# Hybrid diffusion backbone on one core: the output projection by Strassen's method, gating's normalisation on ScalarE, the second modulation in three parts

## The chip, the core and the metric

The kernel runs on one core of a Trainium2 chip. The core has a matmul engine (TensorE, PE in the profile; its weight loads are PEld), a vector engine (VectorE, DVE), a scalar engine (ScalarE, ACT), a general engine (GpSimd, POOL) and a queue that issues DMAs (SyncE, SP). They run side by side and wait for each other by semaphores. The metric is the device time of one execution in microseconds; it is given as a median over several runs.

## The reference

One layer of a token mixer with a convolutional channel mixer, over 512 latent tokens of width 1024 and 256 context tokens. Cut to what matters here:

```python
sh1x, sc1x, g1x, sh2x, sc2x, g2x = split(silu(c) @ w_ada + b_ada, 6)
z = h @ w_in;  u, vs, q, r, ga, gb, k, v, lr = split(z)
a = gelu(u) * (einsum('gpq,bnqgc->bnpgc', sgu_w, layer_norm(gelu(vs))) + sgu_b)   # spatial gating
ob = rms_norm(gated_linear_attention(q, k, v, lr)) * silu(r)
merged = sigmoid(ga) * (a @ w_br_a) + sigmoid(gb) * (ob @ w_br_b)
x = x + g1x * (merged @ w_o)                       # the output projection
hx2 = rms_norm(x) * norm2_g * (1 + sc2x) + sh2x    # second modulation
x = x + g2x * conv_ffn(hx2)                        # up, 3x3 convolution, gelu, down
return rms_norm(x) * final_norm_g
```

The six vectors of the modulation are 1024 long; the first two (sh1, sc1) are made at the start of the kernel, g1, sh2, sc2 and g2 later. `w_ada` is 1024 x 6144.

## The kernel before

All products are made with operands split into a high part (type fp32r) and a low part, and three matmuls for each product: high by high, high by low, low by high. A matmul has a 128 x 128 stationary block and up to 512 moving columns. The high part of a weight is made by ScalarE (L138, `A.copy`), the low part by VectorE (L139, a subtraction); `stream_load` and `stream_split` fetch and split weights some places ahead of their use, in the order of the list `specs`. A raw weight has 4 buffers, a split one 5 (`wh`, `wl`).

The program is written as one sequence. A scheduler of the language orders it for each engine when it is built, by the tiles that the instructions read and write and by the order in the text; an engine then runs its own instructions strictly in that order. Tiles come from pools: `heap` (44 of 2 KB a partition), `late` (27), and the eight PSUM banks as `mm` (4) and `gl` (4). A DMA on SP's queue that needs a tile which isn't free holds up all DMAs behind it.

The stages around the change, in the order in which they run:

- **vs and u.** `wide_tm` makes vs, its gelu is kept in eight `late` tiles `vraw`. After the mean and variance of all tokens are known, 32 operations of VectorE (L1104) write the normalised `vsn`, 128 x 128 each. Then for each of eight column blocks of u: 24 matmuls (`prod_cm`), gelu on ScalarE, and one block later `sgu_part`, the gating with `vsn`.
- **The second modulation** (`ada2`) is a generator that runs in the background: each `tick` takes it one step further. It makes eight accumulators of 512 columns in two parts of four (g1 and sh, then sc and g2). One step fetches a 128 x 512 piece of `w_ada` and adds it, scaled by c, to an accumulator (L1125, VectorE), 32 such steps a part; then each accumulator is split, summed over partitions by two matmuls (L1131, L1132) and copied to a broadcast tile (g1, g2) or turned into a column (sh, sc). Ticks are placed in u, in branch a, in branch b and in the output projection, 80 in all.
- **Branch a** (`wide_kk`, 192 matmuls). Beside it `hx_sums` makes the sums that Strassen's method needs of the input (L1205 to L1226).
- **ga, gb and r** are made by `strassen` on the transposed input: seven products of 24 matmuls in place of eight. The sums of the weights are made partly by DMAs that add into a tile (`add_rows`, POOL's queue), partly by VectorE (L211, L213). In `strassen` a result that takes part in several outputs is copied between banks by ScalarE and combined by VectorE (L453, L459).
- **Branch b** (`wide_tm`, 192 matmuls). Its output tile (t, hf), token tile t of four and column half hf, is multiplied by the gate and added to branch a (L1321, L1322), then put on a list `todo`; `turn` transposes it (four 128 x 128 transposes) and splits it into `mg`, which the output projection reads.
- **The output projection** (`wide_tm`, 192 matmuls). Each output (t, hf) is scaled by g1 and added to x (L1384, L1385), squared and summed on ScalarE (L1386). When both halves of a token tile are there, `norm2_tok` makes its root and scales it, and for each pair of token tiles `norm2_half` transposes (L1371), modulates on ScalarE (L1376) and splits on VectorE (L1379, L1380) into `h2`.
- **Up.** 44 products of 24 matmuls with `h2`. The first four are made on the token half 0 first, 256 columns wide, then on half 1; from block 2 on all 512 columns at once. Behind each pair of products VectorE makes the convolution: eight taps (L1430), then a product with the gelu (L1432). **Down** follows, by Strassen's method too.

Of the kernel before, what the change touches and what calls it, by code (L numbers as in the profile page):

```python
# [8 lines left out]
F32 = mybir.dt.float32  # L9
# [4 lines left out]
ALU = mybir.AluOpType  # L14
# [19 lines left out]
def backbone_kernel(  # L34
# [26 lines left out]
    def late(shape, dt=F32, s="l"):  # L61
        return lp.tile(shape, dt, tag="l", name=nm(s))
# [107 lines left out]

    def w_strassen(w, c0):

# [34 lines left out]
        def split_t2(j):  # L207
            def split():
                r11, r12 = raws["b11k", j], raws["b12", j]
                for kk in range(2):  # L210
                    V.tensor_tensor(tt[j][kk], tt[j][kk], r11[:, kk, :], op=ALU.add)  # L211
# [16 lines left out]
        for o, fs in ((0, [load_raw("b11", 0, 0, j) for j in js]), (2, [load_t(j) for j in js]),  # L228
                      (4, [load_raw("b12", 0, 1, j) for j in js]), (6, [load_raw("b21", 1, 0, j) for j in js]),
                      (10, [load_raw("b22", 1, 1, j) for j in js])):  # L230
            loads.extend((base + o + j, fs[j]) for j in js)
# [18 lines left out]
    w_wide(w_br_b[0], scaled=True)  # L250
    w_wide(w_o[0])
    for f in range(FT):
# [153 lines left out]

    def wide_tm(acts, done, step):
# [3 lines left out]
        for t in range(4):  # L411
            ps = (mm if t else gl)()
# [11 lines left out]
    def strassen(acts, done, step):  # L424

        def prod(ps, name, again):
            for j in range(2):
                wh, wl = weights(3, 6)
                for t in range(2):
                    for kk in range(2):  # L430
                        ah, al = (z[:, t * P:(t + 1) * P] for z in acts[name][2 * j + kk])
                        first = j == 0 and kk == 0 and not again
                        for i, (a, b) in enumerate(((ah, wh), (ah, wl), (al, wh))):
                            T.matmul(ps[t], a, b[:, kk, :], start=(first and i == 0),  # L434
                                     stop=(j == 1 and kk == 1 and i == 2), skip_group_check=again)
                step()
# [664 lines left out]
    vrs, ors = var[:, 0, :], var[:, 1:5, :]  # L1101
    for g in range(8):
        for t in range(4):
            V.tensor_scalar(vsn[g][:, t, :], vraw[g // 4][t][:, (g % 4) * P:(g % 4 + 1) * P], mv[:, t, 0:1],  # L1104
                            vrs[:, t:t + 1], op0=ALU.subtract, op1=ALU.mult)

# [3 lines left out]

    def ada2():
        for part in range(2):
            acc = []
            for j in range(4):
                a_ = late([P, 512], s="acc")
                G.memset(a_, 0.0)
                c0 = 2048 + part * 2048 + j * 512
                dma(a_[0:1, :], b_ada[0:1, c0:c0 + 512])
                acc.append(a_)
            for k in range(KT):  # L1120
                for j in range(4):
                    c0 = 2048 + part * 2048 + j * 512
                    w_ = late([P, 512], s="wa2")
                    dma(w_, w_ada[0, k * P:(k + 1) * P, c0:c0 + 512])
                    V.scalar_tensor_tensor(acc[j], w_, cs[:, k, 0:1], acc[j], op0=ALU.mult, op1=ALU.add)  # L1125
                    yield
            for j in range(4):
                ah, al = split_act(acc[j], s="acc")
                yield
                ps = gl()  # L1130
                T.matmul(ps, ones_r, ah, start=True, stop=False)  # L1131
                T.matmul(ps, ones_r, al, start=False, stop=True)  # L1132
                kind = ("g1", "sh", "sc", "g2")[part * 2 + j // 2]
                if kind in ("g1", "g2"):
                    t_ = late([P, 512], s=kind)
                    A.copy(t_, ps)
                    bc_g[kind, j % 2] = t_
                else:
                    t_ = heap([P, 4, P], s="dg")
                    V.tensor_tensor(t_, ps.rearrange("p (b r) -> p b r", b=4),  # L1140
                                    ident.unsqueeze(1).to_broadcast([P, 4, P]), op=ALU.mult)
                    if kind not in cols:
                        cols[kind] = const([P, 8], "col_" + kind)
                    V.reduce_sum(cols[kind][:, (j % 2) * 4:(j % 2) * 4 + 4], t_, axis=AX.X)
                yield

# [47 lines left out]
    def hx_sums():  # L1194
# [6 lines left out]
        for k in range(4):  # L1201
            u, v = heap([P, 512], s="hu"), heap([P, 512], s="hv")
            s1, q, s3, s4 = u[:, :256], u[:, 256:], v[:, :256], v[:, 256:]
            for d, (h, l), (h_, l_) in ((s1, a22[k], a21[k]), (s3, a11[k], a21[k])):
                V.tensor_tensor(d, f_(h), f_(h_), op=ALU.subtract)  # L1205
                V.tensor_tensor(s4, f_(l), f_(l_), op=ALU.subtract)
# [146 lines left out]

    xs_t = []

    am2 = const([P, 8], "am2")

    def norm2_cols():
        drain()
        V.tensor_scalar(am2, cols["sc"], 1.0, None, op0=ALU.add)  # L1360
        V.tensor_tensor(am2, am2, n2g, op=ALU.mult)
# [19 lines left out]

    def wo_done(hf, t, ps):
        tmp = late([P, 512], s="yt")
        V.tensor_tensor(tmp, ps, bc_g["g1", hf], op=ALU.mult)  # L1384
        V.tensor_tensor(x1[t][hf], x1[t][hf], tmp, op=ALU.add)  # L1385
        A.activation(tmp, x1[t][hf], AF.Square, accum_out=ss2[:, t, hf:hf + 1])  # L1386
        if hf == 1:
            xs_t.append(norm2_tok(t))
            if t >= 2:
                norm2_half(t - 2)  # L1390

    count[0] = 0

    def wo_step():
        count[0] += 1
        do()
        tick(2)
        if count[0] == KT:
            norm2_cols()

    wide_tm(of_blocks(mg), wo_done, wo_step)

# [324 lines left out]
```

## Time and profile before

| | us |
|---|---|
| median of 3 runs | 930.67 |
| runs | 930.3 to 932.23 |
| the profiled execution | 931.34 |
| its span, first to last instruction | 929.6 |

| stage | from, to (us of the span) |
|---|---|
| u, with gating | about 262 to 314 |
| branch a | 314 to 357.6 |
| ga, gb, r | 357.6 to 473.5 |
| branch b | 473.5 to 530 |
| output projection | 530 to 573 |
| up | 573 to 815 |
| down and the final norm | 815 to 929.6 |

The profile is of one execution. Its page gives busy time for each engine, the chain of work that ended last and the costliest groups of instructions by line. Other views of the same trace used below are the waits, the chain in order of time, the timeline of one engine, and windows (busy time of each engine in a stretch, with the clock granted to PE and the share of time that the DMA engines were busy). A row of instructions reads: start, time, engine, line, operation, output<-inputs, count, and in brackets the engine's idle time before it with what ended it.

### The profile page before, as it was taken

To read this page: it belongs to the slowest core of one execution; us is meant where nothing else is said; L and a number is where in the kernel's file an instruction comes from. 1 tells how busy PE (TensorE), PEld (TensorE's weight loads), DVE (VectorE), ACT (ScalarE), POOL (GpSimd) and SP (SyncE) were. 2 spreads that over 40 slices of the span, in tenths; PEclk is the share of its full clock that TensorE was granted. 3 is DMA by queue.
4 is the path that set the end of the run, shared out by engine and by line. 5 is a ranking of instruction groups with operands and counts; after the bars stand their busy time and mean duration, and the time that the engine had idled before them with its cause. 6 is when DMAs were issued, how large, how long until landed. Compare 5 with 4: busy or idle time off the path is not lost.

```text
span 929.6 us, 12825 instructions
## 1 busy us (share of the span) xinstructions
PE 907.7 (98%) x4695; PEld 761.1 (82%) x4695; DVE 755.2 (81%) x1349; ACT 447.8 (48%) x787; POOL 52.8 (6%) x80
## 2 busy tenths in 40 slices
PE   6999999999999999999999999999999999999996
PEld 5776898988878888888878888988888888878885
DVE  5567758689689978866789987798888888999797
ACT  5136546457443337755652334543333333366574
POOL 3000000000000011112100000000000000132000
PEclk9999999999999999999999999999999999999998
DMA  9940411132077384885649642333333333399432
GB/s 275 336 130 24 136 47 46 46 96 64 23 228 231 112 227 90 230 212 144 187 127 340 228 142 78 102 94 95 109 92 91 93 109 110 85 251 246 127 101 91
DMA packets 123547, 130.06 MB, mean 140 GB/s; under 512 B 6953, under 2 KB 84085, under 8 KB 123485
## 3 DMA queue, kind: packets, MB, share of 16 engines
q1 hardware_dynamic: 114781, 115.75, 40.2%
q0 software_dynamic: 6976, 12.28, 8.0%
q10 hardware_dynamic: 1728, 1.22, 0.4%
q8 instruction: 37, 0.61, 0.3%
q14 instruction: 25, 0.20, 0.1%
HBM read 127.13 MB, written 2.10 MB: 139 GB/s over the span
## 4 chain that ended last, share of the span: by engine, by line
PE 82%; DVE 10%; ACT 2%; DMA 2%; issue 2%; SPq 1%; ACTq 0%; DVEq 0%
PE mm L361 27%; PE mm L387 13%; PE gl L434 7%; PE gl L1532 6%; PE mm L434 5%; PE mm L1532 4%; PE gl L387 4%; PE gl L876 3%; PE mm L380 3%; DVE cacc L1430 2%; PE mm L372 1%; PE mm L666 1%; PE mm L980 1%; DVE bc L844 1%; DVE wl L139 1%
## 5 line engine op out<-in xcount | busy, mean ns | idle before, releaser
L138 ACT CAST wh<-raw 128x1024 fp32r<-128x1024 f32 x110 | 115.4, 1052 | 148.8 <-PE mm L361 99.8
L139 DVE TENSOR_TENSOR wl<-raw,wh 128x1024 fp32r<-128x1024 f32 x110 | 133.9, 1220 | 43.7 <-ACT wh L138 43.3
L361 PE MATMUL mm<-h2h,wh 128*128 128x512 f32 (+1 forms) x352 | 133.5, 379 | 0.0
L361 PE MATMUL mm<-h2l,wh 128*128 128x512 f32 (+1 forms) x352 | 133.5, 379 | 0.0
L361 PE MATMUL mm<-h2h,wl 128*128 128x512 f32 (+1 forms) x352 | 133.5, 379 | 0.0
L1430 DVE SCALAR_TENSOR_TENSOR cacc<-ca,ccol,cacc 128x441 f32<-128x441 f32 (+2 forms) x176 | 121.7, 695 | 4.1
L361 PEld LDWEIGHTS mm<-h2h,wh 128*128 128x128 f32 x352 | 66.2, 188 | 12.5
L361 PEld LDWEIGHTS mm<-h2l,wh 128*128 128x128 f32 x352 | 66.2, 188 | 12.4
L361 PEld LDWEIGHTS mm<-h2h,wl 128*128 128x128 f32 x352 | 66.2, 188 | 12.4
L1125 DVE SCALAR_TENSOR_TENSOR acc<-wa,cs,acc 128x512 f32<-128x512 f32 x64 | 45.1, 744 | 2.1 <-DMA wa<-in_w_ada_dram 2.1
L387 PE MATMUL mm<-wh,trh 128*128 128x512 f32 x112 | 44.4, 397 | 0.0
L387 PE MATMUL mm<-wh,trl 128*128 128x512 f32 x112 | 44.0, 392 | 0.0
L387 PE MATMUL mm<-wl,trh 128*128 128x512 f32 x112 | 43.7, 390 | 0.0
L1431 ACT ACTIVATE cacc<-cacc 128x512 f32<-128x512 f32 x22 | 13.9, 633 | 58.5 <-DVE cacc L1430 58.5
L361 PE MATMUL mm<-hxh,wh 128*128 128x512 f32 x104 | 41.7, 401 | 0.0
L361 PE MATMUL mm<-hxh,wl 128*128 128x512 f32 x104 | 41.0, 394 | 0.0
L361 PE MATMUL mm<-hxl,wh 128*128 128x512 f32 x104 | 40.7, 391 | 0.0
L1474 ACT CAST wh<-raw 128x1024 fp32r<-128x1024 f32 x22 | 23.0, 1052 | 20.5 <-PE mm L1532 6.1
L1454 POOL DMA_DIRECT2D b<-in_ffn_w_down_dram x11 | 9.4, 878 | 370.5 <-DMA b<-in_ffn_w_down_dram 356.8
L1475 DVE TENSOR_TENSOR wl<-raw,wh 128x1024 fp32r<-128x1024 f32 x22 | 26.8, 1219 | 4.4 <-ACT wh L1474 4.3
L186 POOL DMA_DIRECT2D tt<-in_w_in_dram x24 | 20.9, 1135 | 166.2 <-DVE hu L1207 77.5
L434 PE MATMUL mm<-wh,hxh 128*128 128x512 f32 x72 | 28.0, 389 | 0.0
(489 smaller groups left out, 2323.5 us busy)
## 6 DMA issues: line engine op xcount, KB each, us to landing
raw<-in_w_in_dram SPq DMA_DIRECT2D x54, 512.0 KB
wa<-in_w_ada_dram SPq DMA_DIRECT2D x96, 256.0 KB
raw<-in_ffn_w_up_dram SPq DMA_DIRECT2D x44, 512.0 KB
raw<-in_ffn_w_down_dram SPq DMA_DIRECT2D x22, 512.0 KB
tt<-in_w_in_dram POOLq DMA_DIRECT2D x24, 256.0 KB, 7.7
raw<-in_w_br_a_dram SPq DMA_DIRECT2D x8, 512.0 KB
raw<-in_w_br_b_dram SPq DMA_DIRECT2D x8, 512.0 KB
raw<-in_w_o_dram SPq DMA_DIRECT2D x8, 512.0 KB
```

What stands on the lines that cost most here:

```text
L138: A.copy(wh, raw)
L139: V.tensor_tensor(wl, raw, wh.bitcast(F32), op=ALU.subtract)
L361: T.matmul(ps, a[:, k, :], b[:, c0:c0 + n], start=(k == 0 and i == 0), stop=(k == KT - 1 and i == 2))
L380: T.matmul(ps, a[:, t * P:(t + 1) * P], b[:, k % 4, :], start=(k == 0 and i == 0), stop=(k == KT - 1 and i == 2))
L387: T.matmul(ps, a, b[:, k % 2, :], start=(k == 0 and i == 0), stop=(k == KT - 1 and i == 2))
L434: T.matmul(ps[t], a, b[:, kk, :], start=(first and i == 0), stop=(j == 1 and kk == 1 and i == 2), skip_group_check=again)
L876: T.matmul(ps, p_, q_, start=(start and z == 0), stop=(stop and z == 2))
L1125: V.scalar_tensor_tensor(acc[j], w_, cs[:, k, 0:1], acc[j], op0=ALU.mult, op1=ALU.add)
L1430: V.scalar_tensor_tensor(o, a_[:, r0 + dy:r1 + dy, c0 + dx:c1 + dx], wcol(tap), o, op0=ALU.mult, op1=ALU.add)
L1474: A.copy(wh, raw)
L1475: V.tensor_tensor(wl, raw, wh.bitcast(F32), op=ALU.subtract)
L1532: T.matmul(ps, a[:, t * P:(t + 1) * P], w[b][:, j, c0:c0 + n], start=(first and i == 0), stop=(last and i == 2), skip_group_check=again)
```

## The change

- The output projection is made by `strassen` in place of `wide_tm`. Its weights come from `w_strassen`, with a new option: b12 + b11 is made by a DMA that adds (`load_b12`), not by VectorE.
- The sums of the merged branches that it needs are made in `mg_turn` behind the same transposes as before, as the outputs of branch b come. For that the second half of branch b goes through the token tiles in the order 2, 0, 3, 1.
- The outputs of the projection now come in the order that `strassen` gives: (t 0, 1; hf 0), (2, 3; 1), (2, 3; 0), (0, 1; 1). The norm of tiles 2 and 3 is therefore made first, and up's first products are made on token half 1 first.
- `vsn` is written by ScalarE, four operations a block, one block ahead of its use, and no longer all at once by VectorE.
- `ada2` runs in three parts: g1 and sh, then sc, both with more ticks in u and branch a and finished before the projection (`drain`), and g2 with one tick a block in up. Its high parts are made by ScalarE.
- `hx_sums` joins high and low parts first (two additions of 512 columns) and then makes its sums, 6 operations a block in place of 10.

```diff
+        def load_b12(j):
+            def load():
+                load_raw("b12", 0, 1, j)()
+                if add_b12:
+                    G.dma_start(raws["b12", j], blk(0, 0, j).rearrange("(k p) c -> p k c", p=P), accum_op=ALU.add)
...
                 w = split_t(j)
-                V.tensor_tensor(r12, r12, raws.pop(("b11k", j)), op=ALU.add)
+                raws.pop(("b11k", j))
+                if not add_b12:
+                    V.tensor_tensor(r12, r12, r11, op=ALU.add)
                 add_rows(j, 1, 0)
...
-    w_wide(w_o[0])
+    w_strassen(w_o[0], 0, True)
...
     A.activation(var, var, AF.Sqrt, bias=eps_t, scale=1.0)
     V.reciprocal(var, var)
     vrs, ors = var[:, 0, :], var[:, 1:5, :]
-    for g in range(8):
+    vnb = const([P, 4], "vnb")
+    V.scalar_tensor_tensor(vnb, mv[:, :, 0], -1.0, vrs, op0=ALU.mult, op1=ALU.mult)
+
+    def vs_norm(g):
         for t in range(4):
-            V.tensor_scalar(vsn[g][:, t, :], vraw[g // 4][t][:, (g % 4) * P:(g % 4 + 1) * P], mv[:, t, 0:1],
-                            vrs[:, t:t + 1], op0=ALU.subtract, op1=ALU.mult)
+            A.activation(vsn[g][:, t, :], vraw[g // 4][t][:, (g % 4) * P:(g % 4 + 1) * P], AF.Identity,
+                         bias=vnb[:, t:t + 1], scale=vrs[:, t:t + 1])
 
 
...
+    def ada2(kinds):
+        cs0 = {"g1": 2048, "sh": 3072, "sc": 4096, "g2": 5120}
+        todo_ = [(kind, j, cs0[kind] + j * 512) for kind in kinds for j in range(2)]
...
+            for a_, (_, _, c0) in zip(acc, todo_):
+                w_ = late([P, 512], s="wa2")
+                dma(w_, w_ada[0, k * P:(k + 1) * P, c0:c0 + 512])
+                V.scalar_tensor_tensor(a_, w_, cs[:, k, 0:1], a_, op0=ALU.mult, op1=ALU.add)
                 yield
...
-    bg.append(ada2())
+    bg.extend([ada2(("g1", "sh")), ada2(("sc",))])
...
-        tick(2)
+        if j < KT - 1:
+            vs_norm(j + 1)
+        tick(2 + j % 2)
...
-            for d, (h, l), (h_, l_) in ((s1, a22[k], a21[k]), (s3, a11[k], a21[k])):
-                V.tensor_tensor(d, f_(h), f_(h_), op=ALU.subtract)
-                V.tensor_tensor(s4, f_(l), f_(l_), op=ALU.subtract)
-                V.tensor_tensor(d, d, s4, op=ALU.add)
-            V.tensor_tensor(q, s1, f_(a11[k][0]), op=ALU.add)
-            V.tensor_tensor(q, q, f_(a11[k][1]), op=ALU.add)
-            V.tensor_tensor(s4, q, f_(a12[k][0]), op=ALU.subtract)
-            V.tensor_tensor(s4, s4, f_(a12[k][1]), op=ALU.subtract)
+            f1, f2 = heap([P, 512], s="hf"), heap([P, 512], s="hf")
+            V.tensor_tensor(f1, f_(hx[k][0]), f_(hx[k][1]), op=ALU.add)
+            V.tensor_tensor(f2, f_(hx[4 + k][0]), f_(hx[4 + k][1]), op=ALU.add)
+            V.tensor_tensor(s1, f2[:, 256:], f1[:, 256:], op=ALU.subtract)
+            V.tensor_tensor(s3, f1[:, :256], f1[:, 256:], op=ALU.subtract)
+            V.tensor_tensor(q, s1, f1[:, :256], op=ALU.add)
+            V.tensor_tensor(s4, q, f2[:, :256], op=ALU.subtract)
...
-            tick(2)
+            tick(3 if count[0] <= KT else 4)
...
+    def mg_turn(t, hf):
+
+        s_, u, f_ = gb[t][hf], t % 2, lambda z: z.bitcast(F32)
+
+        def split(name, src, scale=1.0):
+            hi, lo = heap([P, 512], F32R, s="mh"), heap([P, 512], F32R, s="ml")
+            if scale == 1.0:
+                A.copy(hi, src)
+                V.tensor_tensor(lo, src, f_(hi), op=ALU.subtract)
+            else:
+                A.mul(hi, src, scale)
+                V.scalar_tensor_tensor(lo, src, scale, f_(hi), op0=ALU.mult, op1=ALU.subtract)
+            mg[name, u] = hi, lo
+
+        def go():
+            ps = gl()
+            for kk in range(4):
+                T.matmul(ps[:, kk * P:(kk + 1) * P], s_[:, kk * P:(kk + 1) * P], ident, is_transpose=True,
+                         start=kk == 0, stop=kk == 3, skip_group_check=True)
+            if t > 1 and hf == 0:
+                mf["a21", u] = heap([P, 512], s="mf")
+                A.copy(mf["a21", u], ps)
+            elif hf == 0:
+                mf["a11", u] = heap([P, 512], s="mf")
+                A.copy(mf["a11", u], ps)
+                split("a11", ps)
+                d = heap([P, 512], s="ms")
+                V.tensor_tensor(d, ps, mf["a21", u], op=ALU.subtract)
+                split("s3", d)
+            elif t > 1:
+                split("a22", ps)
+                d, q = mf.pop(("a21", u)), mf["a11", u]
+                V.tensor_tensor(d, ps, d, op=ALU.subtract)
+                V.tensor_tensor(q, q, d, op=ALU.add)
+                split("s2", q, -1.0)
+                split("s1", d)
+            else:
+                split("a12", ps)
+                q = mf.pop(("a11", u))
+                V.tensor_tensor(q, q, ps, op=ALU.subtract)
+                split("s4", q)
+        return go
...
-        todo.append(turn(s_, mg, (t, hf), gl))
+        if hf:
+            todo.append(mg_turn(t, hf))
+        elif t > 1:
+            todo.extend([mg_turn(t, 0), mg_turn(t - 2, 0)])
...
-    wide_tm(of_blocks(ob), br_b_done, br_b_step)
+    wide_tm(of_blocks(ob), br_b_done, br_b_step, (2, 0, 3, 1))
+    drain()
+    am2 = const([P, 8], "am2")
+    V.tensor_scalar(am2, cols["sc"], 1.0, None, op0=ALU.add)
+    V.tensor_tensor(am2, am2, n2g, op=ALU.mult)
...
-    def wo_done(hf, t, ps):
+    def wo_done(hf, t, src, sign):
         tmp = late([P, 512], s="yt")
-        V.tensor_tensor(tmp, ps, bc_g["g1", hf], op=ALU.mult)
-        V.tensor_tensor(x1[t][hf], x1[t][hf], tmp, op=ALU.add)
+        V.tensor_tensor(tmp, src, bc_g["g1", hf], op=ALU.mult)
+        V.tensor_tensor(x1[t][hf], x1[t][hf], tmp, op=ALU.add if sign > 0 else ALU.subtract)
         A.activation(tmp, x1[t][hf], AF.Square, accum_out=ss2[:, t, hf:hf + 1])
-        if hf == 1:
-            xs_t.append(norm2_tok(t))
-            if t >= 2:
-                norm2_half(t - 2)
-
-    count[0] = 0
-
-    def wo_step():
...
+    strassen(lambda name, k, t: [z[:, k * P:(k + 1) * P] for z in mg[name, t]], wo_done, do)
...
-    prods_cm([z[:, :256] for z in pss], ws, h2, 0, 256)
+    prods_cm([z[:, 256:] for z in pss], ws, h2, 256, 256)
     for i in range(4):
-        prod_cm(pss[i][:, 256:], ws[i], h2, 256, 256)
+        prod_cm(pss[i][:, :256], ws[i], h2, 0, 256)
     conv_part(0, pss[0], pss[1])
...
+    bg.append(ada2(("g2",)))
     for f in range(2, FT):
         pa = mm()
         prod_cm(pa, weights(), h2)
         pv = mm()
         prod_cm(pv, weights(), h2)
+        tick()
```

More of the change, by code (lines that the diff above doesn't have):

```diff
@@ L169, in w_wide, with w_strassen @@
                 w_cols(w, hf * 512, 512, 2 * k, 2, scaled)
[L171 removed]
+    def w_strassen(w, c0, add_b12=False):
         base = len(specs)
@@ L186, in add_rows @@
                 G.dma_start(tt[j][kk], blk(kh, nh, j)[kk * P:(kk + 1) * P, :], accum_op=ALU.add)
+        def load_b12(j):
[3 more added lines that the diff above has]
+                    G.dma_start(raws["b12", j], blk(0, 0, j).rearrange("(k p) c -> p k c", p=P), accum_op=ALU.add)
+            return load
         def load_t(j):
@@ L228, in w_strassen @@
         for o, fs in ((0, [load_raw("b11", 0, 0, j) for j in js]), (2, [load_t(j) for j in js]),
-                      (4, [load_raw("b12", 0, 1, j) for j in js]), (6, [load_raw("b21", 1, 0, j) for j in js]),
+                      (4, [load_b12(j) for j in js]), (6, [load_raw("b21", 1, 0, j) for j in js]),
                       (10, [load_raw("b22", 1, 1, j) for j in js])):
@@ L405, in wide_half, with wide_tm @@
             done(hf, t, pss[t])
-    def wide_tm(acts, done, step):
+    def wide_tm(acts, done, step, order=(0, 1, 2, 3)):
         wide_half(0, [mm() for _ in range(4)], acts, done, step)
         ws = [weights() for _ in range(KT // 2)]
-        for t in range(4):
-            ps = (mm if t else gl)()
+        for t in order:
+            ps = (mm if t != order[0] else gl)()
             for k in range(KT):
@@ L430, in prod @@
                     for kk in range(2):
-                        ah, al = (z[:, t * P:(t + 1) * P] for z in acts[name][2 * j + kk])
+                        ah, al = acts(name, 2 * j + kk, t)
                         first = j == 0 and kk == 0 and not again
@@ L1108, in backbone_kernel @@
     bc_g = {}
     cols = {}
[L1111 to L1128, printed above, removed]
-                yield
[L1130 to L1145, printed above, removed]
@@ new lines, in backbone_kernel @@
+    ada_bank = [gl]
+    def ada2(kinds):
+        cs0 = {"g1": 2048, "sh": 3072, "sc": 4096, "g2": 5120}
+        todo_ = [(kind, j, cs0[kind] + j * 512) for kind in kinds for j in range(2)]
+        acc = []
+        for _, _, c0 in todo_:
+            a_ = late([P, 512], s="acc")
+            G.memset(a_, 0.0)
+            dma(a_[0:1, :], b_ada[0:1, c0:c0 + 512])
+            acc.append(a_)
+        for k in range(KT):
+            for a_, (_, _, c0) in zip(acc, todo_):
+                w_ = late([P, 512], s="wa2")
+                dma(w_, w_ada[0, k * P:(k + 1) * P, c0:c0 + 512])
+                V.scalar_tensor_tensor(a_, w_, cs[:, k, 0:1], a_, op0=ALU.mult, op1=ALU.add)
+                yield
+        for a_, (kind, j, _) in zip(acc, todo_):
+            ah, al = split_act(a_, s="acc", eng=A.copy)
+            yield
+            ps = ada_bank[0]()
+            T.matmul(ps, ones_r, ah, start=True, stop=False)
+            T.matmul(ps, ones_r, al, start=False, stop=True)
+            if kind in ("g1", "g2"):
+                t_ = late([P, 512], s=kind)
+                A.copy(t_, ps)
+                bc_g[kind, j] = t_
+            else:
+                t_ = heap([P, 4, P], s="dg")
+                V.tensor_tensor(t_, ps.rearrange("p (b r) -> p b r", b=4),
+                                ident.unsqueeze(1).to_broadcast([P, 4, P]), op=ALU.mult)
+                if kind not in cols:
+                    cols[kind] = const([P, 8], "col_" + kind)
+                V.reduce_sum(cols[kind][:, j * 4:j * 4 + 4], t_, axis=AX.X)
+            yield
@@ L1176, in backbone_kernel @@
     prev = None
+    vs_norm(0)
     for j in range(KT):
@@ L1258, in br_a_step @@
         count[0] += 1
+        if count[0] > KT:
+            ada_bank[0] = mm
         if count[0] % 2:
@@ L1270, in ga_done @@
         V.tensor_tensor(br[t][hf], br[t][hf], sg_, op=ALU.mult)
-    strassen(sums, ga_done, lambda: None)
+    of_sums = lambda name, k, t: [z[:, t * P:(t + 1) * P] for z in sums[name][k]]
+    ada_bank[0] = gl
+    strassen(of_sums, ga_done, lambda: None)
     gb = [[None] * 2 for _ in range(4)]
@@ L1289, in o_scale @@
                 A.mul(os_[t][hf][:, q * 256:(q + 1) * 256], o_tok[h][t // 2][:, t % 2, :], ors[:, h, t:t + 1])
-    strassen(sums, gb_done, o_scale)
+    strassen(of_sums, gb_done, o_scale)
     ob = {}
@@ L1310, in r_step @@
             do()
-    strassen(sums, r_done, r_step)
+    strassen(of_sums, r_done, r_step)
     hx.clear()
@@ L1315, in backbone_kernel @@
     do(len(todo) - 2)
-    mg = {}
+    mg, mf = {}, {}
+    def mg_turn(t, hf):
[31 more added lines that the diff above has]
+                split("s1", d)
+            else:
+                split("a12", ps)
[3 more added lines that the diff above has]
+        return go
     def br_b_done(hf, t, ps):
@@ L1352, in norm2_tok @@
         return xs
[L1354 to L1361, printed above, removed]
+    xs_t = {}
     def norm2_half(hf):
-        bm2 = cols["sh"]
         for k2 in range(4):
@@ L1380, in norm2_half @@
                 V.tensor_tensor(hl, fk, hh.bitcast(F32), op=ALU.subtract)
-    def wo_done(hf, t, ps):
+    def wo_done(hf, t, src, sign):
         tmp = late([P, 512], s="yt")
-        V.tensor_tensor(tmp, ps, bc_g["g1", hf], op=ALU.mult)
-        V.tensor_tensor(x1[t][hf], x1[t][hf], tmp, op=ALU.add)
+        V.tensor_tensor(tmp, src, bc_g["g1", hf], op=ALU.mult)
+        V.tensor_tensor(x1[t][hf], x1[t][hf], tmp, op=ALU.add if sign > 0 else ALU.subtract)
         A.activation(tmp, x1[t][hf], AF.Square, accum_out=ss2[:, t, hf:hf + 1])
-        if hf == 1:
-            xs_t.append(norm2_tok(t))
-            if t >= 2:
-                norm2_half(t - 2)
-    count[0] = 0
-    def wo_step():
[L1395 to L1401, printed above, removed]
+        if hf == (t < 2):
+            xs_t[t] = norm2_tok(t)
+            if t % 2:
+                norm2_half(t // 2)
+    strassen(lambda name, k, t: [z[:, k * P:(k + 1) * P] for z in mg[name, t]], wo_done, do)
     gact, s12, s4 = [], [], []
```

1 line of the change is left out of this document (added).

## The prediction

> **What bounds the kernel now.** First the page's busy line and the chain that ended last, then PE's own waits from the start of branch b to the middle of the down projection.
>
> ```profile
> PE 907.7 (98%) x4695; PEld 761.1 (82%) x4695; DVE 755.2 (81%) x1349; ACT 447.8 (48%) x787; POOL 52.8 (6%) x80
> PE 82%; DVE 10%; ACT 2%; DMA 2%; issue 2%; SPq 1%; ACTq 0%; DVEq 0%
> PE mm L1532 <- DVE cacc L1432: 0.8, 1, 0.8
> ```
>
> PE is busy for 98% of the span, and the one wait shown for it between 473 and 830 us is 0.8 us. A busy PE need not be at its peak, so the next view is the chain in order of time, where a stretch's length over its count is the step from matmul to matmul. The first row is a Strassen product, the others are the end of the output projection.
>
> ```profile
> 368.49 5.44 PE gl L434 x24
> ...
> 549.21 5.47 PE gl L387 x24
> 554.67 10.88 PE mm L387 x48
> 565.56 1.75 PE gl L1371 x16
> 567.30 5.46 PE mm L387 x24
> 572.77 0.22 PE gl L1371 x2
> ```
>
> 24 matmuls of 512 columns take 5.44 us in both forms, 0.227 us each, and between the projection's last matmul and the first ones of up there is no gap: 565.56 + 1.75 = 567.31, 567.30 + 5.46 = 572.76. So the time is PE's matmul count, as long as nobody starves it. Who comes close is read in windows around the change:
>
> ```profile
> 260.00:314.00 54.00, 54.00 (x271) 45.02 (x270) 51.37 (x100) 20.96 (x28) 0.00 (x0) 1.00 0.71 227
> 473.50:517.50 44.00, 43.99 (x210) 35.70 (x208) 40.29 (x65) 13.09 (x22) 0.00 (x0) 1.00 0.73 247
> 517.50:530.00 12.50, 12.50 (x64) 10.43 (x63) 12.42 (x19) 6.37 (x8) 0.00 (x0) 1.00 0.76 267
> 530.00:573.00 43.00, 43.00 (x200) 35.58 (x200) 33.82 (x62) 16.91 (x32) 0.00 (x0) 1.00 0.29 86
> 573.00:586.00 13.00, 13.00 (x109) 12.81 (x109) 11.98 (x33) 7.50 (x16) 0.00 (x0) 1.00 0.57 162
> 801.00:860.00 59.00, 58.20 (x257) 47.90 (x256) 58.67 (x92) 34.71 (x55) 14.54 (x18) 1.00 0.85 205
> ```
>
> Busy times stand in the order PE, PEld, DVE, ACT, POOL. VectorE (DVE) is the second bound: 51.37 of 54 in the stage of u, 12.42 of 12.50 at the end of branch b, 11.98 of 13 at the step into up, 58.67 of 59 from up into down. ScalarE (ACT) has room in all of them.
>
> **The change, part by part.** The sum goes against the profiled run, 931.34 us (span 929.6, 1.74 around it); that is 0.67 above the median, 930.67, and I carry the difference over to the median.
>
> *The product itself.* `wide_tm` issues 8 k x 4 t x 2 halves x 3 = 192 matmuls, `strassen` 7 products x 24 = 168, of the same width. 24 fewer at 5.44 us per 24: **-5.44 us**. The eight turns of four transposes stay eight turns, the 16 matmuls of the modulation only move: 0. The three Strassen projections of before run unbroken, so the form by itself costs PE no wait.
>
> *VectorE around it.* These groups price the rest; the first three are from branch b and the projection, the next three from the Strassen stage, the last two from the stage of u and branch a.
>
> ```profile
> L1125 DVE SCALAR_TENSOR_TENSOR acc<-wa,cs,acc 128x512 f32<-128x512 f32 x32 | 22.1, 743 | 0.0
> L139 DVE TENSOR_TENSOR wl<-raw,wh 128x1024 fp32r<-128x1024 f32 x11 | 13.3, 1217 | 0.0
> L354 DVE TENSOR_TENSOR trl<-gl,trh 128x512 fp32r<-128x512 f32 x12 | 8.0, 683 | 0.8 <-ACT trh L353 0.8
> ...
> L201 DVE TENSOR_TENSOR wl<-tt,wh 128x512 fp32r<-128x512 f32 x36 | 23.0, 684 | 1.5 <-ACT wh L200 1.5
> L211 DVE TENSOR_TENSOR tt<-tt,raw 128x512 f32<-128x512 f32 x12 | 7.8, 685 | 0.0
> L453 DVE TENSOR_TENSOR gl<-gl,es 128x512 f32<-128x512 f32 x6 | 4.0, 692 | 0.4 <-ACT gl L452 0.4
> ...
> L1104 DVE TENSOR_SCALAR vsn<-vr,mv,var 128x128 f32<-128x128 f32 x32 | 8.3, 338 | 0.0
> L1206 DVE TENSOR_TENSOR hv<-hxl,hxl 128x256 f32<-128x256 f32 x4 | 1.7, 419 | 0.0
> ```
>
> From 473.5 to 573, 24 of the 32 L1125 leave (-17.8), and of the eight accumulators' halves and columns two halves and the sc columns stay (-10.2). Added: 14 weight pairs where there were 8, six of them from two 512-wide halves (6 x 1.37 = +8.2), four L211 (+2.7), four combinations like L453 (+2.8), and in `mg_turn` 14 low parts for 8 (+4.1) and eight sums (+5.4). Together 23.2 in, 28.0 out: over both stages VectorE loses some 4.8 us. But it is unevenly spread. In the projection alone I count 13 weight pairs 16.7, L211 2.7, combinations 2.8, six outputs of two operations 8.2, the turns that come last 7.5, two tokens' norm 2.6, two weights of up 2.4: 43, or 39 when each operation gives back the 0.07 by which neighbours overlap, against 38.1 + 0.9 of PE. It starts with no slack.
>
> *The step into up* is where I expect the loss. These rows are one token tile's way through the norm (VectorE), the root's table load and the modulated halves (ScalarE), and the last split halves (VectorE).
>
> ```profile
> 560.15 0.69 DVE L1384 TENSOR_TENSOR yt<-mm,g 128x512 f32<-128x512 f32 x1 [0.54 <-PE mm L387]
> 560.88 0.69 DVE L1385 TENSOR_TENSOR x<-x,yt 128x512 f32<-128x512 f32 x1
> 562.36 0.15 DVE L1347 TENSOR_REDUCE n2s<-ss 128x1 f32<-128x2 f32 x1 [0.79 <-ACT yt L1386]
> 562.88 0.16 DVE L471 RECIPROCAL rstd<-rstd 128x1 f32<-128x1 f32 x1 [0.36 <-ACT rstd L470]
> 563.08 0.88 DVE L1351 TENSOR_SCALAR xs<-x,rstd 128x512 f32<-128x512 f32 x2
> ...
> 556.90 1.28 ACT L470 ACT_TABLE_LOAD   x1
> 581.29 3.76 ACT L1376 ACTIVATE h2f<-gl,col_sh,am 128x256 f32<-128x256 f32 x8 [2.14 <-PE gl L1371]
> ...
> 584.75 0.49 DVE L1379 CAST h2h<-h2f 128x256 fp32r<-128x256 f32 x2
> 585.15 0.75 DVE L1380 TENSOR_TENSOR h2l<-h2f,h2h 128x256 fp32r<-128x256 f32 x2
> ```
>
> A tile's way takes 563.96 - 560.15 = 3.8 us. Before, three tiles are through when the last matmul ends. Afterwards tiles 2 and 3 come after the sixth product and tiles 0 and 1 after the seventh. Tiles 2 and 3 with the table load need about 3.8 + 1.3 = 5.1 us, the seventh product covers 5.44: their transposes just fit. Behind it remain two tiles (2 x 2.4 us of VectorE), 16 split halves (0.53 each, 8.6) and three or four weights of up (3.4 to 4.6), 17 to 18 us, against 3.6 of transposes, 11.5 of up's first halves and about 2.5 until the last k is asked for: 17.6. Bounds: 0 if VectorE never waits; 4 us if it enters 4 us late (43 against 39). Nearest is the window 573 to 586, full and without a PE wait, so I stay below the middle: **+1.8**.
>
> *Gating's normalisation* moves 32 small operations to ScalarE. Before shows no 128-wide one with bias and scale there; below it stands zero, above it the 256-wide L1376, 3.76 / 8 = 0.47, so 0 to 15 us, and I take 0.3 each, 9.6. Its cover is ScalarE's 33 idle us between 260 and 314, one group of four a column block of 6.6 us; without cover it would delay the gelu, and by that the gating matmuls. VectorE gains 8.3 there.
>
> *The modulation, earlier.* Four more L1125 fall into u (+3.0 against -8.3) and four into branch a, with the g1 and sh closings (+8 in all) against hx_sums, which has six 256-wide steps fewer and two 512-wide more a block (4 x (6 x 0.42 - 2 x 0.68) = -4.6). VectorE's net in both is about -1.5. Their DMAs (four more of 256 KB in u, four in a) go on SP's queue ahead of weights that are loaded three ahead: 0, at most +1.
>
> *W_o's loads.* 8 MB instead of 4, the modulation's 6 MB gone from the same stretch; DMA share there is 0.73 to 0.76, so no more than before. The two new accumulating DMAs for b12 stand on POOL's queue between the sums for s3 and those for a22; b12 is multiplied five products later than it is loaded: 0, above it one product, 5.44, if they came late.
>
> *g2 in up.* 16 L1125, one a block, and two closings. Idle time of VectorE per pair of blocks:
>
> ```profile
> 656.49 0.69 DVE L1432 TENSOR_TENSOR cacc<-cacc,mm 128x512 f32<-128x512 f32 x1 [0.76 <-ACT cacc L1431]
> 658.59 1.22 DVE L139 TENSOR_TENSOR wl<-raw,wh 128x1024 fp32r<-128x1024 f32 x1 [1.41 <-ACT wh L138]
> ```
>
> 2 x 0.76 + 1.41 = 2.9 us a pair take in 2 x 0.74. The 16 are done by block 17, but the second closing's low part falls into block 20, where VectorE is full until 860 and PE already waited: +0.6 (0 to 1.2).
>
> **Sum**: -5.44 + 1.8 + 0.6 = -3.0; 931.34 - 3.0 = 928.3 for the profiled run, **927.6** for the median.
>
> **Rivals.**
> - *All hidden.* VectorE catches up in branch b, relieved of 16 L1125. For it: no wait of PE in 517.5 to 530 at 12.42 of 12.50. Then 930.67 - 5.44 = 925.2; chance 0.20.
> - *VectorE becomes the projection's bound*: it enters the step 4 us late, and 4.0 + 0.6 is paid: 929.8, no change that can be measured. For it: 39 to 43 us into 39. Against it: five weight buffers let it run late without PE noticing. Chance 0.15.
> - *PSUM banks.* During the seventh product pairs b and c hold the four gl banks, until the tiles 2 and 3 are read; then two are free for four groups of transposes, and the third group waits for the first one's two h2f, 2 x 0.47, the fourth again: 1.9 more, 929.5. The scheduler can put matmuls between. [...] Chance 0.06.
> - *Slower*: the stall costs clock. Early in the trace PE idles and the clock drops (two matmuls with PE's idle time before them, and a window with the granted clock, 0.51, after the busy times):
>
> ```profile
> 18.50 0.47 PE L666 MATMUL gl<-hxh,qkh 128*128 128x512 f32 x1 [0.69 <-ACT qkh L576]
> 20.86 0.80 PE L666 MATMUL gl<-hxh,qkh 128*128 128x512 f32 x1 [1.89 <-ACT xT L559]
> 20.00:27.00 7.00, 6.14 (x42) 4.40 (x43) 2.31 (x4) 1.29 (x3) 0.00 (x0) 0.51 1.16 306
> ```
>
> 0.69 + 1.89 = 2.6 us idle, then half clock for 7 us, 3.4 us lost. If PE stands 4 us at up's start and the clock falls with it, -5.44 + 4.0 + 3.4 + 0.6 = +2.6: 933.2. [...] Chance 0.13, with any other stall of that size. [...]
>
> **How the numbers follow.** Forecast (926 to 928.8) 0.46, all hidden 0.20, projection bound 0.15, banks 0.06, slower 0.13. 0.2% is 1.9 us, about what a measurement tells from no change: faster 0.66, same 0.21, slower 0.13. The range leaves out most of the slower case and a little of all hidden: 924.9 to 932.0.
>
> **What would show it.** Right: 168 matmuls at L434's line in the projection at 5.44 us per 24; PE gaps only at up's first products and near 825, together 1 to 3.5 us; the normalisation under idle ScalarE; no PE wait in u, a or b. Wrong: gaps of PE inside the seven products, waits of PE or ScalarE on W_o's DMAs, a clock below 1.00 after 570, or VectorE idle for long at the step into up, which would mean that the order and not the work costs.

## The result and the profile after

Changed kernel 942.27 us median (941.65 to 943.36, 4 runs), kernel before 930.48 on the same chip (929.43 to 932.23, 4 runs): ratio 1.0126, 95% interval 1.0108 to 1.0144, **11.8 us slower**. The forecast was 927.6, range 924.9 to 932.0. The profiled execution took 942.39, its span is 940.7.

First the page of the changed kernel: the busy line (engine, busy us, share, instructions) and the engines' shares of the chain that ended last.

```profile
PE 908.0 (97%) x4671; PEld 759.8 (81%) x4671; DVE 761.5 (81%) x1328; ACT 477.6 (51%) x855; POOL 62.1 (7%) x90
...
PE 57%; DVE 30%; issue 5%; ACT 4%; DMA 4%; ACTq 0%; SPq 0%; DVEq 0%; POOL 0%; POOLq 0%
```

24 matmuls fewer (4695 before), as the change says, yet PE's busy time is 0.3 us *more* (907.7 before), and PE's share of the chain fell from 82% to 57%. So PE waits somewhere, and somewhere it runs slowly. PE's waits from the stage of u to the end (waited for: us in total, times, longest):

```profile
PE mm L443 <- ACT wh L207: 7.6, 2, 7.2
PE gl L1434 <- DVE xs L1422: 3.2, 2, 2.0
PE mm L1586 <- DVE cacc L1486: 0.4, 1, 0.4
```

One is inside the seven products (L443), one at the step into up (L1434, the norm's transposes); the third, in down, was 0.8 us before. Windows around both (length; busy us of PE, PEld, DVE, ACT, POOL; PE's granted clock; DMA share; GB/s):

```profile
531.00:534.50 3.50, 3.50 (x17) 2.87 (x16) 3.00 (x6) 2.61 (x5) 0.00 (x0) 1.00 0.15 38
534.50:542.10 7.60, 0.40 (x2) 0.00 (x0) 1.71 (x3) 1.24 (x3) 1.78 (x2) 0.81 0.72 177
542.10:544.00 1.90, 1.85 (x3) 0.79 (x3) 1.29 (x2) 0.78 (x2) 0.28 (x1) 0.50 0.29 51
...
546.00:548.00 2.00, 2.00 (x6) 1.52 (x6) 1.66 (x4) 1.69 (x3) 0.87 (x2) 0.50 0.71 112
548.00:550.00 2.00, 2.00 (x8) 1.56 (x7) 1.74 (x2) 1.47 (x3) 0.80 (x1) 0.63 0.95 204
...
576.00:578.40 2.40, 0.45 (x3) 0.03 (x2) 2.40 (x6) 2.01 (x5) 0.00 (x0) 1.00 0.73 207
578.40:580.00 1.60, 0.83 (x4) 0.40 (x4) 1.60 (x6) 0.86 (x3) 0.00 (x0) 1.00 0.78 230
580.00:582.00 2.00, 1.49 (x7) 1.49 (x8) 2.00 (x5) 1.66 (x7) 0.00 (x0) 0.55 0.43 129
582.00:584.00 2.00, 2.00 (x13) 2.00 (x12) 1.96 (x10) 1.97 (x6) 0.00 (x0) 0.59 0.27 62
```

The bill is read from these rows and from the gaps between the starts of matmuls, less the usual step; such a gap is a little longer than the wait of the view. PE stands 7.4 us in the second product; then 5.9 us at half clock and 2 at 0.63 cost 5.9 x 0.5 + 2 x 0.37 = 3.7. At the step PE stands 2.1 + 1.5 = 3.6 us, and four us at 0.55 and 0.59 cost 1.7. Together **16.4 us**, of the 11.8 + 5.4 = 17.2 that the time came out above a clean gain of the 24 matmuls. VectorE (DVE) isn't full in the first stall: 1.71 of 7.60.

What comes late there is the weights of the product s3 (the tiles tt), second pair. Its way, in the timelines of SP, POOL and ScalarE (start, length, engine, line, operation, output<-input, count; in brackets the idle time before and what ended it):

```profile
492.08 0.93 SPq L199 DMA_DIRECT2D tt<-in_w_o_dram  x2
498.49 34.39 SPq L181 DMA_DIRECT2D raw<-in_w_o_dram  x2
533.00 0.87 SPq L199 DMA_DIRECT2D tt<-in_w_o_dram  x2
...
537.38 1.78 POOL L186 DMA_DIRECT2D tt<-in_w_o_dram  x2 [29.06 <-DMA tt<-in_w_o_dram]
...
541.48 1.14 ACT L207 CAST wh<-tt 128x512 fp32r<-128x512 f32 x2 [5.32 <-DMA tt<-in_w_o_dram]
```

And what SP itself waited for, 480 to 560:

```profile
SPq L181 <- DVE tt L218: 46.6, 2, 33.6
```

The first pair is asked for at 492, the second at 533. Between them two raw loads stand 34 us on SP's queue: b12's second half, which goes at once, and b21's first half, the fifth raw of w_o. There are four raw buffers, held by b11 and b12, and b11 goes free only when VectorE has added it to tt (L218, `split_t2`). So SP waits 33.6 us for that sum, and the second tt pair, which PE needs first, stands behind it.

### The profile page after: what moved, and what is told of

It is laid out like the page before. It is cut to its first block, busy times and chain, and to the rows that moved or that the text cites. A ratio compares the mean times of both kernels' runs of the same rounds, so it can differ in the third digit from the quotient of the medians.

```text
span 940.7 us, 12862 instructions
## 1 busy us (share of the span) xinstructions
PE 908.0 (97%) x4671; PEld 759.8 (81%) x4671; DVE 761.5 (81%) x1328; ACT 477.6 (51%) x855; POOL 62.1 (7%) x90
## 4 chain that ended last, share of the span: by engine, by line
PE 57%; DVE 30%; issue 5%; ACT 4%; DMA 4%; ACTq 0%; SPq 0%; DVEq 0%; POOL 0%; POOLq 0%
PE mm L370 9%; DVE cacc L1484 9%; PE gl L443 7%; PE mm L396 6%; DVE wl L139 6%; PE gl L1586 6%; PE mm L443 5%; PE mm L1586 4%; PE gl L396 3%; PE gl L885 3%; PE mm L389 2%; DVE acc L1138 2%; PE mm L675 2%; ACT wh L138 1%; PE mm L381 1%
## 5 line engine op out<-in xcount | busy, mean ns | idle before, releaser
L139 DVE TENSOR_TENSOR wl<-raw,wh 128x1024 fp32r<-128x1024 f32 x110 | 133.7, 1218 | 36.9 <-ACT wh L138 36.5
L207 ACT CAST wh<-tt 128x512 fp32r<-128x512 f32 x48 | 28.0, 620 | 27.8 <-DMA tt<-in_w_in_dram 8.9
L208 DVE TENSOR_TENSOR wl<-tt,wh 128x512 fp32r<-128x512 f32 x48 | 31.1, 684 | 8.9 <-ACT wh L207 8.8
L443 PE MATMUL mm<-wh,hxh 128*128 128x512 f32 x72 | 28.0, 389 | 0.0
L443 PE MATMUL mm<-wl,hxh 128*128 128x512 f32 x72 | 28.0, 389 | 0.0
L443 PE MATMUL mm<-wh,hxl 128*128 128x512 f32 x72 | 28.0, 389 | 0.0
```

The source lines that it names most:

```text
L139: V.tensor_tensor(wl, raw, wh.bitcast(F32), op=ALU.subtract)
L207: A.copy(wh[:, kk, :], tt[j][kk])
L208: V.tensor_tensor(wl[:, kk, :], tt[j][kk], wh[:, kk, :].bitcast(F32), op=ALU.subtract)
L443: T.matmul(ps[t], a, b[:, kk, :], start=(first and i == 0), stop=(j == 1 and kk == 1 and i == 2), skip_group_check=again)
```

## The experiments

**1. What makes the stall?** Theory A is the one just read: tt's loads stand on SP's queue behind a load that waits. Its rivals: B, tt's own tiles come free late, and the order only shows it; C, POOL's added sums for b12, or the bandwidth, hold tt back; D, VectorE is the projection's bound, as one rival of the forecast had it. Four kernels tell them apart. The first changes the order of two loads and nothing else:

```diff
                 dma(raws[name, j], blk(kh, nh, j).rearrange("(k p) c -> p k c", p=P))
+                if add_b12 and name == "b21":
+                    for i in traced()[at:]:
+                        if i.engine == nc.sync.engine:
+                            tc.add_manual_dep(i, late_tt[-1], mybir.DependencyInfo(
+                                mybir.DependencyClass.NoSync, mybir.DependencyReason.DATA), reason="in_order")
```

> One edit: on SP's queue the load of w_o's b21, first half, is put behind the two loads of the second pair of tt tiles; slots, bytes and all other work stay. Theory A (SP's queue stands at b21's load, which waits for a raw buffer, and tt's loads stand behind it): PE's 7.4 us stall at 534.5 goes and with it the 2.5 us of half clock after it, so 942.3 - 9.9 = 932.4 us (931 to 934). Rival B (the tt tiles' slots come free late, the order is only where it shows): the tt loads then wait at the queue's head for their slots, the stall keeps more than 4 us, 937 or more. Rival C (POOL's added sums for b12, or the bandwidth, hold tt back): the stall stays, 941 to 943. Rival D (VectorE is the projection's bound, as forecast): the gap closes at 534.5 and opens elsewhere in the seven products, 938 or more.

The second takes w_o's tt tiles from the other pool:

```diff
-                tt[j] = [heap([P, 512], s="tt") for _ in range(2)]
+                tt[j] = [(late if add_b12 else heap)([P, 512], s="tt") for _ in range(2)]
```

> One edit: w_o's four tt tiles come from the pool 'late' instead of 'heap'; the second pair is then loaded ahead of b11, in branch b. Theory A and rival B: the stall goes, 932.4 us (930.5 to 934); this run with the one that changes only the order tells A from B. Rival C: the sums for b12 still stand ahead of those for s3 on POOL's queue, and some of the stall stays, 937 or more. Rival D: 938 or more, gaps elsewhere.

The third drops the accumulating loads for b12 (`w_strassen(w_o[0], 0)`):

> One edit: b11 is added to b12 by VectorE, as in the other three Strassen projections, not by POOL's accumulating loads. Theory A and B: SP's order is as it was, the stall stays at 7 us or a little more (four more operations of some 1.2 us on VectorE): 942 to 945 us. Rival C: POOL's queue is free for the sums of s3, the stall goes, 932 to 935. Rival D: VectorE gets 5 us more, 945 or more.

And the fourth makes the change without its projection (the old `wide_tm` for w_o, with the old turns and norm):

> The change without its projection: the output projection, branch b's order and the norm as before; ScalarE's gating normalisation, the modulation in parts with g2 in up, and branch a's sums as after. If the whole loss is in the projection: 930.5 us of before, plus up to 1.2 for g2 and branch a, 930 to 932. By the forecast's own terms for these parts (0 and +0.6): 931.1. If the other parts hold a share of the loss, 933 or more.

| | us | ratio to before, interval |
|---|---|---|
| changed order | 936.62 | 1.0059, 1.0043 to 1.0075 |
| tt from `late` | 935.98 | 1.0056, 1.0040 to 1.0073 |
| b12 on VectorE | 942.92 | 1.0136, 1.0119 to 1.0153 |
| other parts alone | 930.27 | 0.9993, 0.9983 to 1.0002 |

The order of two loads is worth 5.7 us. Giving POOL's added sums for b12 to VectorE (two operations of 1.2 us, not the four expected) wins nothing back, and the parts beside the projection cost nothing that can be measured. The first two missed their 932.4, however. In the kernel with the changed order SP's waits (490 to 535) read:

```profile
SPq L207 <- PE mm L405: 20.5, 1, 20.5
SPq L183 <- DVE tt L227: 20.0, 2, 12.4
```

Now the tt loads stand at the head of the queue (L207 there) and wait 20.5 us for a `heap` tile that branch b's matmuls (L405) still read. That is why the build had put them so late: in the text they come before b12 and b21. They go at 518.5 in place of 533, and PE's stall shrinks to 2.0 us, with one of 0.6 and some half clock behind it. At the step into up PE now waits 4.2 us in place of 3.2.

What is left of the stall is no longer a load. The last added sum for tt is issued by 523.4. In the kernel with tt from `late`, accumulating loads took 5.1 us (tt, median of four) and 6.6 us (one raw) from issue to landing; by the longer of the two it has landed by 530, an estimate. But ScalarE's cast of it stands in ScalarE's queue behind a cast that waits for VectorE, which is busy for 5.00 of the 5 us from 525:

```profile
534.80 0.62 ACT L1353 CAST mh<-mf 128x512 fp32r<-128x512 f32 x1 [1.47 <-DVE mf L1385]
535.32 2.17 ACT L216 CAST wh<-tt 128x512 fp32r<-128x512 f32 x4
```

With tiles from `late`, tt is loaded ahead of b11, all four casts for s3 are done by 525.4, and the stall at 534 is gone. But b21's raw still waits for the sum (SP's longest wait there is 34.8 us), and PE stands 2.2 + 1.0 us at 544, in the fourth product, which uses b21. So A and B are one chain: without a free `heap` tile the build moves the loads back, and there they stand behind a load that waits. Repairing either end of it wins about the same, 5.7 and 6.3 us. One wait on the sum remains in both kernels; only in the second does it stop PE.

**2. A buffer more.** A fifth raw buffer in the changed kernel, nothing reordered by hand:

```diff
-LATE = 27
+LATE = 26
...
-        return wp.tile([P, kn, n], F32, tag="raw", name=nm("raw"), bufs=4)
+        return wp.tile([P, kn, n], F32, tag="raw", name=nm("raw"), bufs=5)
```

> The changed kernel with a fifth raw buffer (pool 'late' one tile smaller, for room); the order at build then puts both halves of b21, the fifth and sixth raw of w_o, ahead of the second pair of tt on SP's queue. Theory A (tt's loads stand behind a raw that waits in SP's queue): the queue stands at the sixth raw instead of the fifth, tt comes as late as before, 941 to 943.5 us. Rival (too few raw buffers, whatever the order): the stall shrinks by half or more, 937 or less.

943.74 us (1.0140, 1.0122 to 1.0158), just above theory A's 941 to 943.5 and far from the rival's 937. PE's stall in the second product is 7.4 us, as before. SP's timeline:

```profile
475.55 15.31 SPq L181 DMA_DIRECT2D raw<-in_w_o_dram  x4
490.91 0.97 SPq L199 DMA_DIRECT2D tt<-in_w_o_dram  x2
497.33 34.40 SPq L181 DMA_DIRECT2D raw<-in_w_o_dram  x2
531.82 0.89 SPq L199 DMA_DIRECT2D tt<-in_w_o_dram  x2
```

The queue now stands at the sixth raw, and tt is as late as before. One buffer more doesn't help, because the build lets one load more go ahead; a sixth buffer wasn't tried.

**3. Taking the wait away.** b11 is added to tt by accumulating loads on POOL's queue, right behind the split for s3, with tt from `late`. Then b11's buffers go free at their split, and no load waits for a sum.

```diff
+        def split_s3(j):
+            def split():
+                w = split_t(j)
+                if add_b12:
+                    add_rows(j, 0, 0)
+                return w
+            return split
...
         def split_t2(j):
             def split():
+                if add_b12:
+                    w = split_t(j)
+                    add_rows(j, 1, 0)
+                    return w
```

> The kernel with w_o's tt tiles in 'late', and b11 added to them by accumulating loads on POOL's queue instead of VectorE: four operations of 0.69 us less on VectorE, and b11's raw buffers are free after their split, so that no load on SP waits for the sum. Theory A: no stall of PE in the seven products, what remains is the step into up: 936.0 - 3.2 (the stall at 544) - 1 to 2 of the step = 931.5 us (929.5 to 933). If the accumulating loads (5 us from issue to landing) come late for the third product: 934 to 938, with PE waiting for wh of tt near 536.

930.77 us (0.9999, 0.9990 to 1.0008). Its chain, in order of time:

```profile
536.58 5.44 PE gl L455 x24
542.01 5.44 PE mm L455 x24
547.46 13.06 PE gl L455 x58
```

The seven products run without a gap, at the 5.44 us for 24 of the forecast's first term. The stall and its half clock (7.4 + 3.7) are gone, and the median is 11.5 below the change. The edit also takes four operations of 0.69 us off VectorE, but that isn't what ended the stop in the fourth product: in the kernel with tt from `late`, VectorE had nothing to do while PE stood there.

```profile
544.00:546.50 2.50, 0.64 (x3) 0.19 (x1) 0.00 (x0) 0.95 (x1) 0.00 (x0) 1.00 1.00 267
```

What still eats the product's gain is the step into up, 1.5 + 1.5 us of gaps.

**4. The step into up.** In the changed kernel VectorE is full there, and its timeline from 569 shows splits of up's weights (L139) between the outputs and the norm of tiles 2 and 3:

```profile
569.51 1.22 DVE L139 TENSOR_TENSOR wl<-raw,wh 128x1024 fp32r<-128x1024 f32 x1
...
571.33 1.23 DVE L139 TENSOR_TENSOR wl<-raw,wh 128x1024 fp32r<-128x1024 f32 x1
...
573.68 1.21 DVE L139 TENSOR_TENSOR wl<-raw,wh 128x1024 fp32r<-128x1024 f32 x1
574.81 0.14 DVE L1418 TENSOR_REDUCE n2s<-ss 128x1 f32<-128x2 f32 x1
574.88 0.68 DVE L1448 TENSOR_TENSOR x<-x,yt 128x512 f32<-128x512 f32 x1
575.48 1.21 DVE L139 TENSOR_TENSOR wl<-raw,wh 128x1024 fp32r<-128x1024 f32 x1
...
577.21 0.15 DVE L480 RECIPROCAL rstd<-rstd 128x1 f32<-128x1 f32 x1
...
577.87 0.87 DVE L1422 TENSOR_SCALAR xs<-x,rstd 128x512 f32<-128x512 f32 x2
```

Two kernels hold the splits of up's first four weights back until tile 3 is normed, on VectorE's queue alone; one on the kernel with the changed order, one on that of experiment 3.

```diff
+            for i in traced()[at:]:
+                if i.engine == nc.vector.engine:
+                    tc.add_manual_dep(i, after_norm[-1], mybir.DependencyInfo(
+                        mybir.DependencyClass.NoSync, mybir.DependencyReason.DATA), reason="in_order")
...
+    specs[UP0:UP0 + 4] = [held_back(z) for z in specs[UP0:UP0 + 4]]
```

> The kernel with the changed order of w_o's loads, and on VectorE the splits of up's first four weights put behind the norm of tiles 2 and 3. Theory 'order' (PE waits at up's start because the weights' splits, 1.2 us each, were put ahead of the norm): the norm comes 3 to 5 us earlier, the 4.7 us of gaps at the step fall under 2.5: 934 us (933 to 935). Theory 'work' (VectorE has more to do there than PE, whatever the order): the gap moves from the transposes to up's first matmuls, which wait for the split weights: 936.6, plus or minus 0.7.

> The one before it, and up's first four weights held behind the norm of tiles 2 and 3. Theory 'order': another 1.5 to 3 us less, 929 us (927.5 to 931). Theory 'work': the same as without the hold, within 0.7.

934.69 us (1.0041, 1.0026 to 1.0056) against 936.62, and 929.49 (0.9985, 0.9976 to 0.9994) against 930.77: 1.9 and 1.3 us less. The first pair doesn't show much: its intervals overlap, and in the profiled executions PE is already ahead before the step, which the hold is about: the clock stayed at 1.00 after the stop at 534, where without the hold it was 0.77, 0.50 and 0.87 over six us (1.7 us). The last section comes back to that. The second pair does: 'order' is right in kind, though the gain is just under its 1.5. There PE's two stops of 1.5 us at the transposes became six of 0.3 to 0.7 at the transposes and up's first matmuls. 'Work' is right too, then: VectorE is in arrears at this place, busy for 11.00 of the 11 us from 565 with the splits held back as well.

Three more, each on the one before it: hold back only the third to fifth weight; load the root's table before the projection; hold ScalarE's casts of these weights as well.

```diff
-    specs[UP0:UP0 + 4] = [held_back(z) for z in specs[UP0:UP0 + 4]]
+    specs[UP0 + 2:UP0 + 5] = [held_back(z) for z in specs[UP0 + 2:UP0 + 5]]
...
+    A.activation(early, am2[:, 0:1], AF.Sqrt, bias=eps_t, scale=0.0)
...
+                if i.engine in (nc.vector.engine, nc.scalar.engine):
```

> The kernel with b11 added by POOL's loads, and only the third to fifth of up's weights held behind the norm of tiles 2 and 3; the first two may fill VectorE's idle time, 3.2 us between 555 and 565 in the run that held all four. Theory 'order': the gaps at the step, 2.7 us with four held, fall to about 1.5: 928.5 us (927.3 to 929.5). Theory 'work': no change, 929.5 plus or minus 0.7.

> The one before it with ScalarE's table for the root loaded ahead of the projection (a root of a constant, whose result is not used), so that the 1.28 us load no longer stands between tile 2's sum and its root. If the norm of tile 2 is the chain that ends last at the step: 0.5 to 1.3 us less than the one before, 927.6 us. If VectorE's queue is: the same within 0.5.

> The one before it with ScalarE's casts for the third to fifth of up's weights (1.05 us each) held behind the root of tile 3 as well. If ScalarE's queue still delays the root: 0.3 to 1 us less than the one before. If not, or if the casts are then late for VectorE's splits: the same, or up to 0.7 us more.

929.66 us (0.9988, 0.9979 to 0.9997), 928.97 (0.9986, 0.9977 to 0.9995) and **927.08** (0.9964, 0.9952 to 0.9977). The first gained nothing, as 'work' had it: PE's waits came back in two larger pieces, 1.5 and 1.3 us. The table may bring 0.7, which these intervals don't prove. The last brought 1.9, about twice the most that was expected; in its profile PE waits for this:

```profile
PE mm L408 <- DVE h2h L1475: 0.7, 1, 0.7
PE mm L408 <- DVE wl L139: 0.5, 1, 0.5
PE mm L1621 <- DVE cacc L1521: 0.4, 1, 0.4
PE gl L1467 <- DVE xs L1453: 0.2, 1, 0.2
```

The gaps at the step add up to 2.0 us in place of 2.5, and the clock stays at 1.00, where the kernel before it ran two us at 0.50, two at 0.82 and two at 0.83 (1.7 us). 0.5 + 1.7 = 2.2 is about the 1.9 gained, and most of it is clock. This kernel beats both: 3.6 us faster than before, 15.2 faster than the change.

## Why the prediction was wrong

- **The product itself, -5.44**: right. 168 matmuls, unbroken at 5.44 us per 24 as soon as the weights are there.
- **The step that failed: "W_o's loads ... 0"**, which cost 11 us (7.4 of stall and 3.7 of half clock), twice the 5.44 of its upper bound. It compared bytes and DMA share, which was indeed lower (0.49 from 473.5 to 517.5, 0.73 before), and asked of POOL's queue only when b12 is needed. It did not lay out SP's queue load by load against the four raw buffers, and it didn't ask in which order the build would put the loads. In its place the runs showed a load of s3's weights standing 33.6 us behind one that waited for a sum. The profile of before had the clue. SP's waits there, 355 to 480, and its timeline show the same wait on the sum, where PE doesn't wait, as all four tt loads of a projection were ahead of it:

```profile
SPq L181 <- DVE tt L211: 45.8, 5, 20.2
```

```profile
400.27 12.53 SPq L181 DMA_DIRECT2D raw<-in_w_in_dram  x5
412.85 1.88 SPq L192 DMA_DIRECT2D tt<-in_w_in_dram  x4
420.31 25.02 SPq L181 DMA_DIRECT2D raw<-in_w_in_dram  x6
```

  The sentence "the form by itself costs PE no wait" was true of those three and does not carry over: the projection's loads come while branch b holds `heap`, and its tt tiles come out of `heap`.
- **The step into up, +1.8 (0 to 4)**: within its bounds where the stall is out of the way (1.5 + 1.5 us of gaps in experiment 3), and 3.6 in the change. What was missing is that two gaps of that size brought the clock down as well, 1.7 us more, which makes 4.7 and 5.3, above the bound. "Just fit" for tiles 2 and 3 was wrong for a reason that was not in that chain: four splits of up's weights stand between the outputs and the norm (L139 from 569.5 to 576.7), where the sum had two in the whole projection and none here.
- **VectorE becomes the projection's bound** (a rival, 929.8): not in the changed kernel, where VectorE has 1.71 us to do in the stall's 7.60. With the loads in another order 2.0 us of the stall remain, and they hang on VectorE by way of ScalarE's queue (experiment 1). At the step into up VectorE is the bound, as experiment 4 shows (11.00 of 11 us).
- **PSUM banks** (a rival, 929.5): in the changed kernel PE's only waits at the transposes are for `xs`, none for `h2f`. With the weights held back there is one of 0.5 us for `h2f`, against 1.9 priced.
- **Slower** (933.2, chance 0.13): right in kind, a stall with the clock at 0.50 behind it, but it sat at another place, and at 7.4 us it was nearly twice the 4 that were priced. Stops in two pieces came with the lower clock too: the 2.6 us early in the trace, from which the 3.4 us of half clock was read, are stops of 0.69 and 1.89, and at the step into up stops of 2.1 and 1.5 us were followed by 0.55 and 0.59.
- **Gating's normalisation, 0**: right as to the time, since the parts beside the projection are the same as before within 0.2%. Its size was low: this group took 482 ns each in the changed kernel, 15 us for 32, and I had taken 0.3. Its cover held, as PE is busy for 54.00 of 54.00 us from 260 to 314 there:

```profile
L1116 ACT ACTIVATE vsn<-vr,vnb,var x32: 478/482/495, 269.6 to 312.4; 128x128 f32<-128x128 f32 x32
```

- **g2 in up, +0.6, and the modulation earlier, 0**: not tested one by one; with the normalisation and branch a's sums they are the -0.6 us, within -1.6 and +0.2, of the parts alone. PE's wait for `cacc` in down, near which the +0.6 was expected, is 0.4 us in the changed kernel and 0.8 before.

## What to carry to other kernels

When a stage gets other loads, write its queue down load by load, with the buffer that each load needs and the instruction that frees it: in the change one load that waited 33.6 us held back the tt loads behind it, which PE needed first. Do this on the order that the build has made: with no free `heap` tile the tt loads came behind that load, and went at 533 in place of 518.5. And price a stop of PE together with the lower clock that may come with it: in experiment 3 gaps of 3.0 us cost 4.7.

## What was not expected of the hardware

A stop of PE far shorter than the 7.4 us above, 2.0 us, was followed by a clock of 0.50 in one kernel and not in another. Both kernels with the changed order of loads stop for 2.0 us at the same place, at 534. Windows of the first, without the hold:

```profile
533.70:536.00 2.30, 0.45 (x3) 0.03 (x2) 1.62 (x3) 1.20 (x3) 0.00 (x0) 1.00 0.43 163
536.00:538.00 2.00, 1.69 (x4) 0.80 (x5) 2.00 (x5) 1.49 (x3) 0.36 (x1) 0.77 0.00 0
538.00:540.00 2.00, 2.00 (x6) 1.62 (x6) 1.92 (x4) 0.82 (x2) 1.33 (x2) 0.50 0.45 68
```

And of the second, with the hold, which stops again for 2.1 us at the step:

```profile
533.80:536.10 2.30, 0.46 (x4) 0.04 (x2) 1.62 (x3) 1.20 (x3) 0.00 (x0) 1.00 0.37 142
536.10:538.00 1.90, 1.45 (x4) 0.66 (x4) 1.90 (x5) 1.51 (x3) 0.26 (x1) 1.00 0.00 0
538.00:540.00 2.00, 1.89 (x8) 1.59 (x9) 1.91 (x5) 0.71 (x2) 1.44 (x2) 1.00 0.28 35
...
566.60:569.00 2.40, 0.43 (x3) 0.04 (x1) 0.90 (x4) 2.39 (x4) 0.00 (x0) 1.00 0.00 0
569.00:571.00 2.00, 2.00 (x9) 1.39 (x10) 2.00 (x6) 0.31 (x1) 0.00 (x0) 0.68 0.00 0
571.00:573.00 2.00, 2.00 (x11) 1.77 (x10) 1.94 (x3) 1.65 (x4) 0.00 (x0) 0.50 0.00 1
```

After the stop at 534 the clock is 0.77 and 0.50 in the one kernel and stays at 1.00 in the other, so in these two its length alone didn't decide. The two drops come 2.9 and 2.7 us after the stop began (0.77 over two us is 0.92 us at half, 0.68 is 1.28). In the change's stop of 7.4 us the drop comes about 4.3 us after, while PE still stands (0.75 in the half us from 539.0, 0.50 from 539.5). PE pays while it is fully busy: 2.00 of 2.00 us at 0.50, with 6 matmuls from 538 where the second kernel has 8. Two stops of 1.5 us with 0.8 of work between them did the same in experiment 3 (0.69 and 0.50 in the four us from 567), and the six of 0.3 to 0.7 us did not (1.00 throughout). What decides between 2.0 us with and without a drop isn't settled by these runs.
